# Row sums by ScalarE, a bias added by DMA, a diagonal that turns and scales, and eight dot products in a later stage

## The chip, the cores and the metric

The kernel runs on one core of a Trainium2 chip. The metric is the time of one execution on the device in microseconds, lower is better. The core has five engines that run side by side and meet through semaphores: TensorE (matrix products into PSUM), VectorE, ScalarE (activations, copies with a scale), GpSimd, and SyncE, whose queue (SP) issues most loads. DMAs are issued from the queues of SP, ScalarE and GpSimd.

## The reference

One decoder block over 512 positions with 1024 channels. Two token mixers run on one normed input; the parts that matter here, shortened:

```python
z = h @ w_in                      # a_u, a_v, q, k, v, index parts, gates A and B
mod = silu(c) @ w_ada + b_ada     # six vectors of 1024: shift, scale, gate, twice

# mixer A: gated spatial mixing in chunks of 128 positions, 8 groups
v = layer_norm(gelu(a_v), ln_g, ln_b).reshape(bsz, n, 128, 8, 128)
mixed = einsum('gts,bnsgc->bntgc', w_s * tril, v) + b_s
y_a = gelu(a_u) * mixed

# mixer B: attention over the top 128 keys of an indexer, 8 heads of 128
p = softmax(q @ k_selected);  o = p @ v_selected
merged = sigmoid(g_a) * (y_a @ w_proj_a) + sigmoid(g_b) * (y_b @ w_proj_b)
x = x + gate1 * (merged @ w_out)  # then a SwiGLU block and a norm
```

With the layer norm's offset `ln_b` taken through the mixing, its share is `ln_b` times the row sum of the masked weights; the kernel adds it to the bias.

## The kernel before, in words

The program is one straight list of instructions per engine; their order is that of the calls in the code, without loops on the chip and without a scheduler. The stages follow each other: a first projection (0 to 60 us of the span), q, k, v and the indexer (to 104), a_v (to 156), a_u (to 206), gate A and projection A (to 291), attention together with gate B (to 373), projection B, output projection and the feed-forward block.

Most products run in a split form: an fp32 operand is cut into a high part (ScalarE copies with rounding) and a low part (VectorE or GpSimd subtracts), and `mm3` makes three matmuls of them, high by high, high by low, low by high. Weights come as a list `stream` of 512 KB entries, in the order in which they are made ready. `issue` starts an entry's load into one of three `raw` buffers (`RAWB = 3`), and `room` lets it do so when fewer than three are pending; `prep` makes the high and low part. `get(i, ahead)` makes everything ready up to `ahead` weight chunks further on. A chunk of a_u or gate B has 4 x 128 rows by 256 columns, 24 matmuls of 512 columns.

Between the weight entries stand 24 dot-product entries (kind "m") that make three of the six modulation vectors: rows of `w_ada` are loaded and VectorE forms, in one instruction per 128 outputs (line 209), their product with silu(c) and its sum. `group(..., mods=mm_, nm=...)` puts `nm` of them behind each chunk. With a tile name in `mraw` such an entry has a buffer of its own; with `mraw=False` it shares the three `raw` buffers.

In a_u (`au_tasks` ahead of each chunk's get, `au_post` after its matmuls) VectorE ends the statistics of a_v, ScalarE normalises a_v (`ln_v2`), TensorE makes the mixing products (`mix_mm`, plain fp32), and VectorE combines them with the bias tile `bsb` and with gelu(a_u) (`mix_ev`). The bias tile is loaded by GpSimd as a broadcast to all partitions; the row sums come from a product with a tile of ones (`rs_mm`), and eight VectorE instructions (`bias_mix`) add them, times `ln_b`, to the bias. GpSimd's queue also issues the moves and adding moves of `x_move`, which form sums of weight blocks in DRAM.

In attention there are 16 units of two heads by one block of 128 queries, with four, three, two and one block of keys in turn. In step s unit s has its qk products, mask, maxima (line 1183) and exponentials, unit s-1 its normalisation, unit s-2 is turned (`at_T`) and unit s-3 has its products with v. Between them `gb_part` puts one or two of gate B's 32 steps.

## Time and profile before

| | |
|---|---|
| runs shown | 791.23, 791.38 and 862.42 us, median 791.38 |
| the profiled execution | 791.98 us, its span 790.0 us |
| busy share of the span | TensorE 99%, VectorE 84%, ScalarE 56%, GpSimd 23% |
| DMA | 155.05 MB, mean 196 GB/s |
| granted TensorE clock | 1.00 in each stretch looked at |

The span runs from the first to the last instruction of the program; the execution's own time is 2.0 us longer. A busy share is the time in which an engine has at least one instruction running, over the span. Matmuls overlap each other in the record, so for TensorE the distance between the starts of two neighbours says more than the length of one.

### The profile page before, as it was taken

How to read it: one execution, taken by the hardware profiler on the slowest of the kernel's cores; microseconds unless marked ns; L12 is line 12 of the kernel's file. 1: busy time of each engine (PE TensorE's matmuls, PEld its weight loads, DVE VectorE, ACT ScalarE, POOL GpSimd, SP SyncE). 2: the span in 40 equal slices, each digit the busy share in tenths (PEclk: the TensorE clock that was granted, in tenths of full speed). 3: DMA queues.
4: the chain of work that ended last, by engine and by line, in shares of the span. 5: the costliest groups of instructions: out<-in, count | busy, mean ns of one | idle time of the engine just before them, and what ended most of it. 6: DMA issues, size and time to landing. Idle time of an engine off the chain costs nothing.

```text
span 790.0 us, 12600 instructions
## 1 busy us (share of the span) xinstructions
PE 778.3 (99%) x4747; PEld 694.5 (88%) x4747; DVE 663.7 (84%) x1114; ACT 443.2 (56%) x777; POOL 181.4 (23%) x220
## 2 busy tenths in 40 slices
PE   8999999999999999999999999999999999999996
PEld 6779988878988988988888899999999999878885
DVE  5988887688897799886787879889999888898777
ACT  6556455443362636666536577555665566576654
POOL 2064234574353501000010000313121322100001
PEclk9999999999999999999999999999999999999999
DMA  9959454789763733148692503989998968666664
GB/s 361 416 156 242 119 146 122 217 231 243 212 215 107 235 112 107 54 135 278 232 234 56 187 1 107 255 251 268 258 259 222 260 201 212 177 200 209 209 192 147
DMA packets 89887, 155.05 MB, mean 196 GB/s; under 512 B 7010, under 2 KB 54770, under 8 KB 89635
## 3 DMA queue, kind: packets, MB, share of 16 engines
q1 hardware_dynamic: 72976, 116.05, 44.6%
q0 software_dynamic: 15952, 37.17, 20.9%
q10 hardware_dynamic: 898, 1.04, 0.4%
q8 instruction: 37, 0.61, 0.3%
q14 instruction: 24, 0.19, 0.1%
HBM read 150.16 MB, written 33.56 MB: 233 GB/s over the span
## 4 chain that ended last, share of the span: by engine, by line
PE 64%; DVE 17%; DMA 9%; ACT 5%; issue 4%; POOL 0%; SPq 0%; POOLq 0%; ACTq 0%; DVEq 0%
PE R L66 5%; PE R L68 5%; PE R L67 5%; PE pb L66 5%; PE pb L67 5%; PE pb L68 5%; DMA mraw<-in_w_ada_t_dram 3%; DMA raw<-in_w_ffn_in_dram 3%; DMA raw<-in_w_ffn_out_dram 3%; PE pfo L67 2%; PE pfo L68 2%; PE pfo L66 2%; PE pav L66 2%; PE pav L67 2%; PE pav L68 2%
## 5 line engine op out<-in xcount | busy, mean ns | idle before, releaser
L134 ACT ACTIVATE hi<-raw 128x1024 fp32r<-128x1024 f32 (+1 forms) x111 | 114.5, 1032 | 81.6 <-PE pb L67 32.4
L138 DVE TENSOR_TENSOR lo<-raw,hi 128x1024 fp32r<-128x1024 f32 (+2 forms) x77 | 90.3, 1174 | 26.9 <-ACT hi L134 26.0
L138 POOL TENSOR_TENSOR lo<-raw,hi 128x1024 fp32r<-128x1024 f32 x27 | 69.5, 2577 | 100.2 <-ACT hi L134 69.6
L67 PE MATMUL pfo<-lo,za 128*128 128x512 f32 (+1 forms) x144 | 55.5, 386 | 0.2 <-DVE lo L138 0.2
L66 PE MATMUL pfo<-hi,za 128*128 128x512 f32 (+1 forms) x144 | 55.5, 385 | 0.0
L68 PE MATMUL pfo<-hi,za 128*128 128x512 f32 (+1 forms) x144 | 55.3, 384 | 0.0
L209 DVE CUSTOM_DVE_ANT_0 mraw<-mraw,scb,cols 128x1024 f32<-128x1024 f32 x24 | 37.6, 1568 | 11.7 <-DMA mraw<-in_w_ada_t_dram 11.7
L66 PE MATMUL R<-tb,sx 128*128 128x256 f32 x160 | 45.0, 281 | 0.3 <-ACT gr L462 0.3
L67 PE MATMUL R<-tb,sx 128*128 128x256 f32 x160 | 44.3, 277 | 0.0
L68 PE MATMUL R<-tb,sx 128*128 128x256 f32 x160 | 44.3, 277 | 0.0
L68 PE MATMUL R<-tb,lo 128*128 128x256 f32 x160 | 44.2, 277 | 0.0
L67 PE MATMUL R<-tb,hi 128*128 128x256 f32 x160 | 44.2, 276 | 0.0
L66 PE MATMUL R<-tb,hi 128*128 128x256 f32 x160 | 44.2, 276 | 0.0
L66 PE MATMUL pb<-h,hi 128*128 128x512 f32 (+1 forms) x112 | 42.7, 382 | 0.0
L68 PE MATMUL pb<-h,lo 128*128 128x512 f32 (+1 forms) x112 | 41.9, 374 | 0.0
L67 PE MATMUL pb<-h,hi 128*128 128x512 f32 (+1 forms) x112 | 41.9, 374 | 0.0
L351 POOL COPY sm<-sm 128x1 f32<-128x1 f32 x36 | 23.2, 644 | 78.7 <-ACT sm L350 78.7
L331 POOL DMA_DIRECT2D wsum<-in_w_ffn_out_dram x24 | 21.2, 885 | 78.0 <-DMA wsum<-wsum 46.1
L66 PEld LDWEIGHTS pfo<-hi,za 128*128 128x128 f32 x144 | 27.1, 188 | 6.1 <-ACT ps L1925 0.6
L67 PEld LDWEIGHTS pfo<-lo,za 128*128 128x128 f32 x144 | 27.1, 188 | 6.1 <-DVE lo L138 0.9
L68 PEld LDWEIGHTS pfo<-hi,za 128*128 128x128 f32 x144 | 27.1, 188 | 5.2
L66 PEld LDWEIGHTS R<-tb,sx 128*128 128x128 f32 x160 | 30.1, 188 | 0.9 <-ACT gr L462 0.5
(398 smaller groups left out, 2697.0 us busy)
## 6 DMA issues: line engine op xcount, KB each, us to landing
raw<-in_w_ffn_in_dram SPq DMA_DIRECT2D x44, 512.0 KB, 5.7
raw<-in_w_in_dram SPq DMA_DIRECT2D x30, 512.0 KB, 3.8
wsum<-in_w_ffn_out_dram POOLq DMA_DIRECT2D x30, 512.0 KB, 8.3
mraw<-in_w_ada_t_dram SPq DMA_DIRECT2D x24, 512.0 KB, 6.3
raw<-wsum SPq DMA_DIRECT2D x20, 512.0 KB, 3.8
s<-in_w_ada_t_dram SPq DMA_DIRECT2D x16, 512.0 KB, 8.8
raw<-in_w_ffn_out_dram SPq DMA_DIRECT2D x16, 512.0 KB, 4.6
xsum<-in_w_blocks_dram POOLq DMA_DIRECT2D x12, 512.0 KB, 6.3
```

What stands on the lines that cost most here:

```text
L66: T.matmul(o, wh, rh, start=start, stop=False, **kw)
L67: T.matmul(o, wh, rlo, start=False, stop=False, **kw)
L68: T.matmul(o, wlo, rh, start=False, stop=stop, **kw)
L134: A.activation(hi[:, :m], e["raw"][:, :m], AF.Copy)
L138: e["lo"].tensor_sub(lo[:, :m], e["raw"][:, :m], f(hi[:, :m]))
L209: V.tensor_tensor_reduce(out=raw[:, o], in0=raw[:, o], in1=c, scale=1.0, scalar=col if o.start else bias, op0=OP.mult, op1=OP.add, accum_o ...
L331: P.dma_start(wsum[n][o], src, accum_op=OP.add)
L351: P.tensor_copy(t, t)
```

## The change

Three things are changed.

1. The row sums of the masked spatial weights are made by ScalarE from a second copy of the weights (`gmlp_w_n`, positions in rows; loaded and masked by GpSimd), as the accumulated sum of eight copies. TensorE turns the eight columns, ScalarE copies them out and writes them to DRAM, GpSimd loads them back as a broadcast, ScalarE scales them by `ln_b`, and a DMA of GpSimd adds the bias on top. `rs_mm`, the tile of ones and `bias_mix` are gone.
2. In attention the weights after the exponential are no longer scaled by VectorE. ScalarE makes a diagonal matrix of the inverse sums (`at_diag`, two 128x128 instructions per unit), and the turn is a product with that diagonal in place of a transpose with the identity.
3. The eight dot products that stood between a_u's chunks are gone from there; gate B has two behind each chunk in place of one. All 24 keep their order, so those behind the chunks of projection A are now of the first modulation vector and those of gate B follow on.

```diff
--- before.py
+++ after.py
@@ -27,7 +27,7 @@
 
 @with_exitstack
 def block_kernel(ctx: ExitStack, tc: tile.TileContext, x, x_t, c_row, positions, w_ada_t, w_first, w_in, w_blocks,
-                 gmlp_w_s, gmlp_b_s, w_proj_a, w_proj_b,
+                 gmlp_w_s, gmlp_w_n, gmlp_b_s, w_proj_a, w_proj_b,
                  w_out, w_ffn_in, w_ffn_out, final_norm_g, small, consts, out):
     nc = tc.nc
     T, V, A, P, SY = nc.tensor, nc.vector, nc.scalar, nc.gpsimd, nc.sync
@@ -256,7 +256,7 @@
     mm_ = mods_mid()
     dram = ctx.enter_context(tc.tile_pool(name="dram", bufs=1, space=bass.MemoryType.DRAM))
     W_AV = [[add_w(w_in, [k0, k0 + 1], 1024 + 512 * h, 512, V if k0 % 4 else P) for k0 in range(0, 8, 2)] for h in range(2)]
-    W_AU = [group(w_in, 256 * g, pool=2, mods=mm_, mraw="acc") for g in range(4)]
+    W_AU = [group(w_in, 256 * g, pool=2) for g in range(4)]
     xsum = {(r, n): dram.tile([128, 1024], F32, name=f"xsum{r}{n}") for r in range(2) for n in (1, 2, 3, 4)}
 
     def blk(r, k):
@@ -281,7 +281,7 @@
             W_X[r].append(add_w(b, [0, 1, 2, 3], 0, 256, V if p in (2, 5) else P, 48 if p in (1, 4) else 16))
         for g in (2 * r, 2 * r + 1):
             W_PA.append(group(w_pa, 256 * g, mods=mm_, pool=True, nm=(1 - g % 2,) * 2, mraw=("A2", "A3") if g % 2 == 0 else "A2"))
-    W_GB = [group(w_in, 5192 + 256 * g, pool=2 * (g == 1), mods=mm_, nm=1, mraw=False)
+    W_GB = [group(w_in, 5192 + 256 * g, pool=2 * (g == 1), mods=mm_, nm=2, mraw=False)
             for g in range(4)]
     stream[W_GB[1][0]]["lo"] = V
     W_PB = [group(w_pb, 256 * g, mods=mm_, nm=((0, 1), (1, 1), (1, 0), (0, 0))[g], mraw="k_hi") for g in range(4)]
@@ -296,6 +296,7 @@
     KZ = ([0, 1, 2, 3, 4, 5, 6, 7, 12, 13, 20], [8, 9, 10, 11, 16, 17, 18, 19, 14, 15, 21])
     NZ = 6
 
+    rsd = dram.tile([8, 128], F32, name="rsd")
     wsum = {n: dram.tile([11 * 128, 512], F32, name=f"wsum{n}") for n in (1, 2, 3, 4)}
     gdr = {n: dram.tile([8, 128], F32, name=f"gdr{n}") for n in (2, 5)}
     W_Z = {}
@@ -887,10 +888,37 @@
     vg = []
     late = {}
 
-    def load_bs():
+    def load_wn():
+        late["wn"] = mid.tile([128, 8, 128], F32, name="wn", tag="A1", bufs=1)
+        P.dma_start(late["wn"], gmlp_w_n)
+
+    def mask_wn():
+        P.affine_select(late["wn"], late["wn"], pattern=[[0, 8], [-1, 128]], compare_op=OP.is_ge, fill=0.0, base=0,
+                        channel_multiplier=1)
+
+    def row_sums():
+        for g in range(8):
+            w = late["wn"][:, g]
+            A.activation(w, w, AF.Copy, accum_out=sm[:, g:g + 1])
+
+    def rs_out():
+        p = bank(4, "rsT")
+        T.transpose(p[:8, :128], sm[:, 0:8], ident)
+        gr = tiny.tile([128, 128], F32, name="gr", tag="gr", bufs=1)
+        A.activation(gr[:8], p[:8, :128], AF.Copy)
+        A.dma_start(rsd, gr[:8])
+
+    def rs_in():
         late["bsb"] = mid.tile([128, 8, 128], F32, name="bsb", tag="A3", bufs=1)
-        P.dma_start(late["bsb"], bass.AP(tensor=gmlp_b_s.tensor, offset=gmlp_b_s.offset,
-                                         ap=[[0, 128], [128, 8], [1, 128]]))
+        P.dma_start(late["bsb"].rearrange("p a n -> p (a n)"), rows_bcast(rsd, D))
+
+    def rs_scale():
+        for m in range(8):
+            b = late["bsb"][:, m]
+            A.activation(b, b, AF.Copy, scale=lnbc[:, m:m + 1])
+
+    def add_bs():
+        P.dma_start(late["bsb"].rearrange("p a n -> p (a n)"), rows_bcast(gmlp_b_s, D), accum_op=OP.add)
 
     def load_ws():
         late["wmT"] = mid.tile([128, 8, 128], F32, name="wmT", tag="A2", bufs=1)
@@ -899,15 +927,13 @@
     def mask_ws():
         P.affine_select(late["wmT"], late["wmT"], pattern=[[0, 8], [1, 128]], compare_op=OP.is_ge, fill=0.0, base=0,
                         channel_multiplier=-1)
-        late["ones"] = mid.tile([128, 2, 128], F32, name="ones2", tag="ql", bufs=2)[:, 0]
-        P.memset(late["ones"], 1.0)
 
     VT = {0: [load_ws, lambda: rows_a(1), lambda: rows_b(1)],
-          1: [lambda: h_hi("S1"), lambda: h_hi("S4"), lambda: h_lo("S1"), lambda: h_lo("S4")],
+          1: [load_wn, lambda: h_hi("S1"), lambda: h_hi("S4"), lambda: h_lo("S1"), lambda: h_lo("S4")],
           2: [lambda: rows_a(2), lambda: rows_b(2), lambda: h_hi("S3")],
-          3: [lambda: h_lo("S3")],
-          5: [mask_ws],
-          7: [load_bs]}
+          3: [lambda: h_lo("S3"), mask_wn],
+          4: [row_sums],
+          5: [mask_ws]}
     for _ in range(16):
         bg.append((1.4, topk_max))
         bg.append((1.4, topk_replace))
@@ -940,6 +966,8 @@
             for tk in range(4):
                 opt_a_mm(pb[tk], tk, hi, lo, stream[i]["kts"], hT, 8)
             idx_mms(4 if vs > 2 else 3)
+            if vs == 7:
+                rs_out()
         if not vg:
             vg.extend(mid.tile([128, 2, D], F32, name=f"vg{i}", tag=f"P{i}", bufs=1) for i in range(2))
         for tk in range(4):
@@ -980,17 +1008,6 @@
             ylow.append(lambda: V.tensor_sub(yT[m][1], y, f(yT[m][0])))
         ylate.append((austep[0] - 1, hi))
 
-    def rs_mm():
-        late["rs"] = [bank(5 + k, "rs") for k in range(2)]
-        for k, p in enumerate(late["rs"]):
-            T.matmul(p, late["ones"], late["wmT"][:, 4 * k:4 * k + 4].rearrange("p a n -> p (a n)"), start=True, stop=True)
-
-    def bias_mix():
-        for m in range(8):
-            b = late["bsb"][:, m]
-            V.scalar_tensor_tensor(b, late["rs"][m // 4][:, 128 * (m % 4):128 * (m % 4) + 128], lnbc[:, m:m + 1], b,
-                                   op0=OP.mult, op1=OP.add)
-
     ub = {}
     austep = [0, 0]
     AT = {3: [0], 4: [1, 2], 5: [3], 6: [4], 7: [5], 8: [6], 9: [7]}
@@ -998,8 +1015,6 @@
     def au_post():
         s = austep[1]
         austep[1] += 1
-        if s == 2:
-            rs_mm()
         for m in AT.get(s, []):
             mix_mm(m)
         while ylate and ylate[0][0] < s:
@@ -1014,11 +1029,14 @@
                 ln_v(tk, 1)
             rstd(rva, mva[:, :, 1], 4, 1.0)
             V.scalar_tensor_tensor(nmr, mva[:, :, 0], -1.0, rva, op0=OP.mult, op1=OP.mult)
+            rs_in()
         elif s < 3:
+            if s == 1:
+                rs_scale()
+            else:
+                add_bs()
             ln_v2(2 * s - 2)
             ln_v2(2 * s - 1)
-        elif s == 3:
-            bias_mix()
         while ylow:
             ylow.pop(0)()
         for m in AT.get(s - 1, []):
@@ -1198,8 +1216,16 @@
         n = (i + 1) * 128
         pt, mx = AS["p", u]
         V.reciprocal(mx[:, 6:8], mx[:, 4:6])
+
+    dgs = []
+
+    def at_diag(u):
+        if not dgs:
+            dgs.append(base.tile([128, 4, 2, 128], F32, name="dg", tag="hs4", bufs=1))
+        mx = AS["p", u][1]
+        AS["d", u] = dgs[0][:, u % 4]
         for e in range(2):
-            V.tensor_scalar(pt[e][:, :n], pt[e][:, :n], mx[:, 6 + e:7 + e], None, op0=OP.mult)
+            A.activation(AS["d", u][:, e], ident, AF.Copy, scale=mx[:, 6 + e:7 + e])
 
     def at_T(u):
         i, hp = aun[u]
@@ -1213,8 +1239,8 @@
             p = bank(4 + s0 // 2, "pT")
             for s in range(ns):
                 for e in range(2):
-                    T.transpose(p[:, (s * 2 + e) * 128:(s * 2 + e + 1) * 128],
-                                pt[e][:, (s0 + s) * 128:(s0 + s + 1) * 128], ident)
+                    T.matmul(p[:, (s * 2 + e) * 128:(s * 2 + e + 1) * 128],
+                             pt[e][:, (s0 + s) * 128:(s0 + s + 1) * 128], AS["d", u][:, e], start=True, stop=True)
             o = th[:, s0:s0 + ns].rearrange("p s e n -> p (s e n)")
             ol = tl[:, s0:s0 + ns].rearrange("p s e n -> p (s e n)")
             ev.append((o, ol, p[:, :ns * 256]))
@@ -1277,6 +1303,8 @@
         low = at_split(s + 2, True) if 0 < s < NU - 2 else lambda: None
         if s < NU:
             at_exp(s)
+        if 1 <= s <= NU:
+            at_diag(s - 1)
         low()
         gb_part(GBN[s], 2 if s else 1)
     mbank[0] = 6
...
     given["gmlp_w_s"] = _np.asarray(inputs["gmlp_w_s"])[0].transpose(2, 0, 1)
+    given["gmlp_w_n"] = _np.asarray(inputs["gmlp_w_s"])[0].transpose(1, 0, 2)
     for name in _INS:
         a = _np.ascontiguousarray(given[name])
         arrays[f"in_{name}_dram"] = a
```

On ScalarE, at the start of a_u: the rows from the high part of a_u's second chunk (the first row) to the high part of its fourth (the last). `vg` is a_v, `pav` its PSUM banks, `bsb` the bias tile.

```order
L134 ACTIVATE hi<-raw 128x1024 [waits DMAHW2_49,Pool_49]
L946 ACTIVATE vg_1305<-pav 128x512 [waits PE_49] x2
L946 ACTIVATE vg_1306<-pav 128x512 [waits PE_49] x2
L134 ACTIVATE hi<-raw 128x1024 [waits DMAHW4_49]
L952 ACTIVATE vg_1305<-vg_1305,sm 128x1024 [waits DVE_49,Activation_49]
L952 ACTIVATE vg_1305<-vg_1305,sm 128x1024 [waits Activation_49]
L134 ACTIVATE hi<-raw 128x1024 [waits DMAHW5_49,PE_49]
```

And in the changed kernel:

```order
L134 ACTIVATE hi<-raw 128x1024 [waits DMAHW2_49,Pool_49]
L974 ACTIVATE vg_1309<-pav 128x512 [waits PE_49] x2
L974 ACTIVATE vg_1310<-pav 128x512 [waits PE_49] x2
L134 ACTIVATE hi<-raw 128x1024 [waits DMAHW3_49]
L918 ACTIVATE bsb<-bsb,cols 128x128 [waits DMASW0_49]
L918 ACTIVATE bsb<-bsb,cols 128x128 x7
L980 ACTIVATE vg_1309<-vg_1309,sm 128x1024 [waits DVE_49,Activation_49]
L980 ACTIVATE vg_1309<-vg_1309,sm 128x1024 [waits Activation_49]
L134 ACTIVATE hi<-raw 128x1024 [waits DMAHW4_49,PE_49]
```

The eight scalings, which wait for the broadcast's DMA, stand ahead of two normalisations and of the fourth chunk's high part.

On SP's queue, from the last load of projection A to the fifth load of gate B's stage; `raw<-in_w_in` is a weight chunk of gate B, `raw<-in_w_ada` a dot-product entry.

```order
L115 DMA raw<-in_w_proj_a_dram 128x4x256 [waits DMAHW6_49,Pool_49]
L205 DMA mraw<-in_w_ada_t_dram 128x1024
L115 DMA raw<-in_w_in_dram 128x4x256 [waits DMAHW7_49,DVE_49]
L205 DMA raw<-in_w_ada_t_dram 128x1024 [waits DMAHW1_49,Pool_49]
L115 DMA raw<-in_w_in_dram 128x4x256 [waits DMAHW2_49,DVE_49]
L205 DMA raw<-in_w_ada_t_dram 128x1024 [waits DMAHW4_49,DVE_49]
L115 DMA raw<-in_w_in_dram 128x4x256 [waits DMAHW0_49,DVE_49]
```

And in the changed kernel:

```order
L115 DMA raw<-in_w_proj_a_dram 128x4x256 [waits DMAHW6_49,Pool_49]
L205 DMA mraw<-in_w_ada_t_dram 128x1024
L115 DMA raw<-in_w_in_dram 128x4x256 [waits DMAHW7_49,DVE_49]
L205 DMA raw<-in_w_ada_t_dram 128x1024 [waits DMAHW1_49,Pool_49]
L205 DMA raw<-in_w_ada_t_dram 128x1024 [waits DMAHW2_49,DVE_49]
L115 DMA raw<-in_w_in_dram 128x4x256 [waits DMAHW4_49,DVE_49]
L205 DMA raw<-in_w_ada_t_dram 128x1024 [waits DMAHW0_49,DVE_49]
```

The second weight chunk of gate B is the fourth load into the three buffers, where it was the third; its wait on VectorE is that for the low part of the first chunk.

On VectorE, from the low part of gate B's first chunk (the first row) to the first unit's maxima (the last rows, `pt,mx<-qk`):

```order
L138 TENSOR_TENSOR lo<-raw,hi 128x1024
L773 TENSOR_SCALAR sco_639<-sco_639 128x384
L773 TENSOR_SCALAR sco_638<-sco_638 128x256
L1070 TENSOR_TENSOR ql<-qf_615,qh 128x256
L209 ISA raw,Gc<-raw,scb,cols 128x1024
L209 ISA Gc 128x1
L138 TENSOR_TENSOR lo<-raw,hi 128x1024
L1183 ISA pt,mx<-qk,sco_640 128x512
```

And in the changed kernel:

```order
L138 TENSOR_TENSOR lo<-raw,hi 128x1024
L774 TENSOR_SCALAR sco_640<-sco_640 128x384
L774 TENSOR_SCALAR sco_639<-sco_639 128x256
L1088 TENSOR_TENSOR ql<-qf_616,qh 128x256
L209 ISA raw,GG_88<-raw,scb,cols 128x1024
L209 ISA GG_88 128x1
L209 ISA raw,GG_88<-raw,scb,cols 128x1024
L209 ISA GG_88 128x1
L138 TENSOR_TENSOR lo<-raw,hi 128x1024
L1201 ISA pt,mx<-qk,sco_641 128x512
```

A second dot product stands ahead of the second chunk's low part, and the first unit's maxima stand behind that low part in both.

## Rows read from the trace of the kernel before

**Rows 1.** The page, busy times of the engines (us, share of the span, instructions):

```profile
PE 778.3 (99%) x4747; PEld 694.5 (88%) x4747; DVE 663.7 (84%) x1114; ACT 443.2 (56%) x777; POOL 181.4 (23%) x220
```

**Rows 2.** Stages: length, PE, PEld, DVE, ACT, POOL busy, clock, DMA share, GB/s:

```profile
110.00:155.00 45.00, 44.98 (x209) 37.74 (x208) 33.77 (x47) 22.55 (x40) 22.71 (x23) 1.00 0.60 156
155.00:222.00 67.00, 67.00 (x383) 58.29 (x383) 55.69 (x98) 30.06 (x40) 34.39 (x22) 1.00 0.80 221
...
290.00:372.00 82.00, 81.89 (x482) 72.39 (x481) 69.53 (x203) 51.31 (x128) 5.59 (x5) 1.00 0.45 146
```

**Rows 3.** Waits of TensorE's matmuls, longest first (us in total, times, longest):

```profile
PE warm L492 <- POOL ones L382: 2.4, 1, 2.4
...
PE zx L1116 <- DVE zx L1126: 0.4, 1, 0.4
```

**Rows 4.** Timeline of TensorE around the ones-product (start, us, engine, line, names):

```profile
172.04 0.39 PE L68 MATMUL pb<-h,lo 128*128 128x512 f32 x1
172.27 1.88 PE L986 MATMUL rs<-wmT,ones 128*128 128x512 f32 x4
...
174.22 0.40 PE L67 MATMUL pb<-h,hi 128*128 128x512 f32 x1
```

**Rows 5.** The same around the first mixing product:

```profile
179.48 1.05 PE L965 MATMUL mix<-wmT,vg 128*128 128x128 f32 x8
...
180.60 0.40 PE L67 MATMUL pb<-h,hi 128*128 128x512 f32 x1
```

**Rows 6.** The same around one unit's transposes:

```profile
311.00 1.04 PE L1216 MATMUL pT<-ident,pt 128*128 128x128 f32 x8
...
312.10 0.39 PE L67 MATMUL pgb<-h,hi 128*128 128x512 f32 x1
```

**Rows 7.** Groups of VectorE, 290 to 372 us (count, busy us, mean ns, idle before):

```profile
L1202 DVE TENSOR_SCALAR pt<-pt,mx 128x512 f32<-128x512 f32 (+3 forms) x32 | 10.9, 384 | 0.6
L209 DVE CUSTOM_DVE_ANT_0 raw<-raw,scb,cols 128x1024 f32<-128x1024 f32 x8 | 10.2, 1280 | 0.0
```

**Rows 8.** Timeline of ScalarE, exponentials of a unit with one key block:

```profile
351.71 0.40 ACT L1193 ACTIVATE pt<-pt,mx 128x128 f32<-128x128 f32 x1
352.02 0.19 ACT L1193 ACTIVATION_READ_ACCUMULATOR pt<-pt,mx 128x1 f32 x1
352.11 0.39 ACT L1193 ACTIVATE pt<-pt,mx 128x128 f32<-128x128 f32 x1
```

**Rows 9.** Timeline of ScalarE and GpSimd at the start of a_u:

```profile
159.10 1.13 POOL L268 DMA_DIRECT2D xsum<-in_w_blocks_dram  x1
...
159.42 2.38 ACT L952 ACTIVATE vg<-vg,sm 128x1024 f32<-128x1024 f32 x2 [1.73 <-DVE sm L1016]
...
170.91 2.40 POOL L138 TENSOR_TENSOR lo<-raw,hi 128x1024 fp32r<-128x1024 f32 x1 [4.30 <-ACT hi L134]
```

**Rows 10.** DMA issues (queue, count, KB each, median us from issue to landing):

```profile
xsum<-in_w_blocks_dram POOLq DMA_DIRECT2D x12, 512.0 KB, 6.3
...
raw<-in_w_ada_t_dram SPq DMA_DIRECT2D x8, 512.0 KB, 4.4
...
bsb<-in_gmlp_b_s_dram POOLq DMA_DIRECT2D x1, 512.0 KB, 5.1
```

**Rows 11.** Timeline of SP's queue, ScalarE, VectorE and TensorE at gate B's start:

```profile
283.82 0.37 SPq L115 DMA_DIRECT2D raw<-in_w_in_dram  x1
...
287.60 1.06 ACT L134 ACTIVATE hi<-raw 128x1024 fp32r<-128x1024 f32 x1 [5.81 <-DMA raw<-in_w_in_dram]
...
288.40 0.34 SPq L205 DMA_DIRECT2D raw<-in_w_ada_t_dram  x1
...
290.30 1.23 DVE L138 TENSOR_TENSOR lo<-raw,hi 128x1024 fp32r<-128x1024 f32 x1
...
292.20 0.69 DVE L1183 CUSTOM_DVE_ANT_0 pt<-qk,sco 128x512 f32<-128x512 f32 x1 [0.68 <-PE qk L68]
...
294.04 0.39 PE L66 MATMUL qk<-k_hi,qh 128*128 128x512 f32 x1
```

More of the change, by code (lines that the diff above doesn't have):

```diff
@@ L2026, in block_kernel @@
                 finish(tk)
-_INS = ["x", "x_t", "c_row", "positions", "w_ada_t", "w_first", "w_in", "w_blocks", "gmlp_w_s", "gmlp_b_s",
+_INS = ["x", "x_t", "c_row", "positions", "w_ada_t", "w_first", "w_in", "w_blocks", "gmlp_w_s", "gmlp_w_n", "gmlp_b_s",
         "w_proj_a", "w_proj_b", "w_out", "w_ffn_in", "w_ffn_out", "final_norm_g", "small", "consts"]
```

## The prediction

> **What bounds the kernel now.** I read the busy times first, then the stages, then what TensorE waited for, then single rows at the places the diff touches. TensorE is busy for 778.3 us, 99% of the span [rows 1], in the two stages concerned for 67.00 of 67.00 and 81.89 of 82.00 us, at a granted clock of 1.00, while VectorE has 55.69 and 69.53 [rows 2]. Busy time alone could hide stretched matmuls, so the second look is at waits: once the first projection runs, no wait of a matmul is longer than 0.4 us, and that one is on the sum of a Strassen block [rows 3]. The third look is at starts: 512-column matmuls start 0.23 us apart, right up to the next kind of work [rows 4]. So TensorE's issue is the limit, stage by stage. Work taken off VectorE or ScalarE is worth nothing where no matmul waits for it; work put on TensorE costs its full length; a new wait costs what exceeds its slack. I therefore price TensorE rows in full and everything else by slack.
>
> **Turning with the diagonal.** The two scalings per unit leave VectorE: 32 rows, 10.9 us of its time [rows 7]. ScalarE makes 32 diagonals, 128x128, instead; the nearest row is the exponential of that shape, 0.31 us up to its accumulator read [rows 8], so 9.9 us on an engine with 51.31 of 82 us busy. The transposes become real matmuls of fp32 data. A transpose is one row of the trace: 80 rows for 80 blocks, 8 of them from 311.00 until the next 512-column matmul but one, 312.10, less its 0.23, so 311.87: 0.109 us each [rows 6]. The spatial mixing has the same shape, fp32 by fp32; the code makes four calls per group and the trace has eight rows, from 179.48 to 180.60 - 0.23 = 180.37, 0.111 us each [rows 5]: a true fp32 product is two rows. TensorE therefore gets 160 x 0.111 - 80 x 0.109 = 17.8 - 8.7 = **+9.1 us**, all on the path that sets the end, with no cover. This is the largest term and the best founded one.
>
> **Row sums.** The ones-product goes: four rows from 172.27 to 174.22 - 0.23 = 173.99, **-1.7 us** on TensorE [rows 4]. One 8-column transpose comes, at most one row of the turning kind, +0.1. The eight combinations that leave VectorE are no gain by themselves. On ScalarE the eight row sums are 8 x 0.40 = 3.2 us [rows 8] at step 4 of a_v; it is busy for 22.55 of 45 us in that stretch, so the relu rows behind them move into pauses: 0 to 0.5 us, I take 0. The masking of the second copy is one more pass on GpSimd, which has 22.71 us to do there [rows 2]. The sums' way through DRAM ends before GpSimd reaches the broadcast.
>
> The new wait is in a_u. GpSimd issues the broadcast where it now issues a weight-sum move, 159.10 [rows 9]; the bias load of the same size took 5.1 us [rows 10], so it lands near 164.2. ScalarE stands waiting in front of it, and behind it in its queue are two normalisations and the high part of a_u's fourth chunk. 8 x 0.31 = 2.5 us of scaling end at 166.7, the two normalisations take 2.4, to 169.1, the high part 1.06 [rows 11], to 170.1, GpSimd's low part 2.40, to 172.5. TensorE comes to that chunk at 172.27 (where the ones-product stood) and to its low part two matmuls later, at 172.7. So the slack of some 8 us that these steps had is just used up: nothing with these values, 1.0 us with the broadcast at the 6.3 us of GpSimd's other moves [rows 10]. I take **+0.2**. The adding DMA stands behind that low part on GpSimd, with a weight-sum move and the next low part behind it; at 6.3 us it lands near 179, when its reader's other input, the first mixing product at 179.48 [rows 5], is only being made: 0.
>
> **The dot products.** VectorE loses 8 x 1.28 us in a_u and the waits for their loads, and gets as many back in gate B [rows 7], where 10.9 us have left. The 0.4 us wait at the end of a_u, behind late VectorE work [rows 3], should go: **-0.4**, between 0 and twice that.
>
> What is dear is the order of the loads. The three raw buffers take gate B's first chunk, then two dot-product rows, and the second weight chunk must wait until the first chunk's low part has freed a buffer. Its load was issued at 283.82 and used at 287.60; now it takes the place of the load at 288.40 [rows 11]. With the same 3.8 us it lands at 292.2, its high part ends at 293.3, its low part (1.23) at 294.5. VectorE stands in front of that low part, and behind it is the first unit's softmax, which started at 292.20. Its first half (0.69) reads the bank that the second unit's qk wants: that started at 294.04 and can now start at 294.5 + 0.7 = 295.2, **+1.2 us**. The first turn also comes later, since its diagonal stands on ScalarE behind the second unit's exponentials: of the 2.3 us by which the softmax is late TensorE has then lost 1.2, so up to 1.1 us more, **+0.4** if a good half of that was slack. Together 1.6; with a load of 3.0 us 0.8, with one of 6.3 us 4.1. From then on a unit has more TensorE work and no more VectorE work, so the pipeline catches up and I expect nothing further. Later loads have a whole chunk's time.
>
> **Sum.** 9.1 - 1.7 + 0.1 + 0.2 - 0.4 + 1.6 = +8.9 us. The profiled execution took 791.98 us (790.0 of span and 2.0 around it), so 800.9; the runs shown at 791.23 and 791.38 are some 0.6 lower: **800.3 us**, 1.1% above the median.
>
> **A rule weighed.** The rows say that TensorE has no room in the attention stage: 81.89 of 82.00 us busy and no wait over 0.4 us [rows 2, 3]. The Trainium skill, Perfetto Trace Analysis, section Identifying the Most-Contended Engine, says that matmul busy time measures the nearness to the limit badly, and that the busy share of the weight loads does it well. By that rule 72.39 of 82.00 us leave 9.6 us of room in the stage, and the sum would be 800.3 - 9.1 = 791.2. I trust the starts of the matmuls: 481 weight loads in 72.39 us are 0.15 us each, under the 0.23 us of a 512-column stream, so full issue already shows as less than full load time.
>
> **Rivals.** *The extra TensorE rows fit into pauses* (chance 0.07). For it: VectorE had 85% of the stage, and with 10.9 us off it the units could close up. Against: rows 2, 3 and 4. The 9.1 us fall away, 791.2, and if the late start is absorbed too, 789.6. This is where the rule above would lead.
>
> *The diagonal product is one row per block, as the transpose was* (0.04), so that the change costs less than the code seems to say. For it: same shape, same stationary operand. Against: two rows per call in the mixing. Price: again without the 9.1, 791.2.
>
> *Loads in gate B bind chunk after chunk* (0.07), the case that ends slower by over 2%. Place: the raw buffers, where a chunk's load starts only after the last chunk's low part. Cycle: landing + 1.06 + 1.23. Per chunk TensorE has 24 x 0.23 = 5.5 us of gate and two units; counted in rows of 0.11 us, a unit with one key block has 11 of them and a chunk there 7.9 us, one with two blocks 20 and 9.9 us, and the mean over the stage is (82.0 + 9.1) / 8 = 11.4. At 3.8 us of landing the cycle is 6.1 and hides; it decides from 5.6 us on in the shortest units. At 10 us it is 12.3 and costs 2 x 4.4 + 2 x 2.4 = 13.6 us more, 813.9. For it: 24 loads instead of 16 in this stage, and moves of 6.3 us elsewhere. Against: a DMA share of 0.45 in the stage [rows 2], and dot-product loads that land in 4.4 us there [rows 10].
>
> **How the numbers follow.** The forecast has 0.82, the rivals 0.07, 0.04 and 0.07. The low end takes 0.8 off for the wait at the end of a_u, 0.8 for the start and 0 in a_u: 9.1 - 1.7 - 0.8 + 0.1 + 0.8 = 7.5, 798.8; I set it at 797, for small stretches of matmuls in the attention stage that VectorE's relief may shorten and that no row sums up. The high end takes 0.5 in a_v, 1.0 in a_u, 4.1 at the start and no gain on the wait: 9.1 - 1.7 + 0.1 + 0.5 + 1.0 + 4.1 = 13.1, 804.4, with the same margin up 806. Range **797 to 806**. Two per cent, about what a measurement of this kernel tells from no change, is 15.8 us, 807.2: slower by over that 0.07, faster by over that 0.01, within 0.92.
>
> **What would show it.** Right: 160 rows of the turning product, about 0.111 us apart; no rows of the ones-product; a VectorE with more idle time in a_u and as much work as before in gate B; one wait of about 1 us at the second unit's qk, with load, high part, low part and softmax before it; the fourth chunk of a_u with no wait above 1 us. Wrong: 80 turning rows, or an attention stage lengthened by much less than 9 us; waits of TensorE spread over all chunks of gate B; a span that shrinks though TensorE's rows grew.

## The result, and the profile after

The changed kernel took 801.4 us in the median of four runs (801.31 to 802.36), the kernel before 791.6 on the same chip: a ratio of 1.0128, 95% interval 1.0108 to 1.0148, so 9.8 us more. One of the four runs of the kernel before took 862.42 us; it counts in that median and not in the ratio. 800.3 was predicted. The profiled execution has a span of 800.4 us, 10.4 more than before.

The page's busy times:

```profile
PE 786.6 (98%) x4824; PEld 703.7 (88%) x4824; DVE 653.4 (82%) x1074; ACT 456.8 (57%) x834; POOL 182.8 (23%) x222
```

The stages of [rows 2], with the same columns:

```profile
110.00:156.00 46.00, 44.54 (x208) 37.30 (x207) 34.62 (x43) 25.02 (x56) 23.36 (x23) 1.00 0.54 136
156.00:223.00 67.00, 67.00 (x392) 59.15 (x391) 46.42 (x82) 33.57 (x49) 36.57 (x25) 1.00 0.76 197
290.00:383.00 93.00, 91.28 (x558) 80.81 (x557) 66.85 (x185) 61.58 (x162) 4.63 (x5) 1.00 0.51 165
```

TensorE has 77 rows more than in [rows 1]: 80 for the turn, one transpose of the sums, less the four of the ones-product. The attention stretch is 93 us long here and was 82 in [rows 2]; both begin and end at chosen whole microseconds, and the starts of the matmuls, below, give 12.1 us of growth. In a_u VectorE lost 9 us of work and TensorE stayed full. TensorE now has pauses in a_v and in attention, which the waits name (us in total, times, longest):

```profile
PE pav L66 <- ACT vg L974: 1.5, 1, 1.5
PE pv L67 <- DVE tl L1300: 1.1, 2, 0.6
...
PE pT L1242 <- ACT dg L1228: 0.4, 1, 0.4
```

The `zx` wait of [rows 3] is gone. The turn of one unit, in the timeline of TensorE (start, us, engine, line, names):

```profile
313.01 1.95 PE L1242 MATMUL pT<-dg,pt 128*128 128x128 f32 x16
314.80 0.27 PE L461 MATMUL mod<-ident,GG 128*8 128x128 f32 x1
```

Where [rows 6] had eight rows there are sixteen, and the next start is 1.79 us later: 0.112 us a row, close to the 0.111 that the prediction took from the mixing.

**The a_v pause.** Rows of GpSimd, VectorE, ScalarE and TensorE (a bracket holds the idle time before and what ended it):

```profile
113.79 0.57 POOL L893 DMA_DIRECT2D wn<-in_gmlp_w_n_dram  x1
...
115.03 1.00 POOL L753 MEMSET sco<- 128x512 f32 x1
...
126.96 2.08 POOL L896 TENSOR_SCALAR_AFFINE_SELECT wn<-wn 128x1024 f32<-128x1024 f32 x1
...
128.00 2.44 DVE L754 SCALAR_TENSOR_TENSOR sco<-rl,wi,sco 128x512 f32<-128x512 f32 x2
...
132.43 2.07 ACT L974 ACTIVATE vg<-pav 128x512 f32<-128x512 f32 x4
133.08 0.50 PE L66 MATMUL pav<-hi,h 128*128 128x512 f32 x1 [1.46 <-ACT vg L974]
```

The two VectorE rows in the kernel before:

```profile
127.15 1.60 DVE L753 SCALAR_TENSOR_TENSOR sco<-rl,wi,sco 128x512 f32<-128x512 f32 x2
```

The issue of the second copy's load takes GpSimd 0.57 us, and behind it stands a fill for which VectorE's index sums wait: 1.91 us, where it was 1.34. Then the mask runs beside two rows of those sums, which take 2.44 us in place of 1.60. 0.57 and 0.84 make 1.41; ScalarE's gelu is late by about that, and TensorE waits 1.46 us for PSUM banks. The 0.84 is taken up by an experiment below; the 0.57 is read from this trace alone, since no kernel here has the load's issue elsewhere.

**a_u.** ScalarE at the fourth chunk, GpSimd behind it:

```profile
165.32 2.45 ACT L918 ACTIVATE bsb<-bsb,cols 128x128 f32<-128x128 f32 x8 [5.82 <-DMA bsb<-rsd]
167.68 2.37 ACT L980 ACTIVATE vg<-vg,sm 128x1024 f32<-128x1024 f32 x2
169.95 1.04 ACT L134 ACTIVATE hi<-raw 128x1024 fp32r<-128x1024 f32 x1
...
171.07 2.41 POOL L138 TENSOR_TENSOR lo<-raw,hi 128x1024 fp32r<-128x1024 f32 x1 [5.38 <-ACT hi L134]
173.42 0.92 POOL L921 DMA_DIRECT2D bsb<-in_gmlp_b_s_dram  x1
```

The prediction had these steps at 164.2, 166.7, 169.1 and 170.1; they came up to 1.1 us late, but so did TensorE after a_v, and no matmul waits.

**Attention's ends.** SP's queue, ScalarE, VectorE and TensorE, first at the start and then at the end of the stage:

```profile
286.94 0.38 SPq L115 DMA_DIRECT2D raw<-in_w_in_dram  x1
...
290.49 1.06 ACT L134 ACTIVATE hi<-raw 128x1024 fp32r<-128x1024 f32 x1 [9.46 <-DMA raw<-in_w_in_dram]
...
292.72 0.68 DVE L1201 CUSTOM_DVE_ANT_0 pt<-qk,sco 128x512 f32<-128x512 f32 x1
...
293.56 0.47 PE L66 MATMUL qk<-k_hi,qh 128*128 128x512 f32 x1
...
361.85 1.53 SPq L205 DMA_DIRECT2D raw<-in_w_ada_t_dram  x2
364.19 7.93 SPq L115 DMA_DIRECT2D raw<-in_w_proj_b_dram  x3
...
372.47 1.06 ACT L134 ACTIVATE hi<-raw 128x1024 fp32r<-128x1024 f32 x1 [2.03 <-DMA raw<-in_w_proj_b_dram]
373.56 1.23 DVE L138 TENSOR_TENSOR lo<-raw,hi 128x1024 fp32r<-128x1024 f32 x1 [1.84 <-ACT hi L134]
...
374.70 0.42 DVE L1290 TENSOR_TENSOR yb<-pv,yb 128x256 fp32r<-128x256 f32 x1
...
375.65 0.42 DVE L1300 TENSOR_TENSOR tl<-pT,th 128x256 fp32r<-128x256 f32 x1
...
376.12 0.39 PE L67 MATMUL pv<-tl,v_hi 128*128 128x256 f32 x1 [0.50 <-DVE tl L1300]
```

At the start the load that [rows 11] had at 283.82 comes at 286.94, the first maxima 0.52 us later than there, the second unit's qk 0.48 earlier. At the end the first chunk of projection B is issued behind two dot-product loads and lands 8.3 us after its issue. ScalarE waits 2.03 us in front of its high part, VectorE 1.84 us in front of its low part. Behind that low part VectorE has, without a gap, `yb` of a finished unit, the maxima of another and then `tl`, for which TensorE waits. ScalarE's copies behind the high part end at 374.1, before `tl` starts, so here the lateness passes through VectorE's queue.

The starts of the same matmuls in both traces, after minus before, show where the time goes: +0.26 us since the start-up, +1.80 at the end of a_v, +0.04 past the place of the ones-product, -0.75 in gate A, +11.37 at the end of attention, +10.44 near the end of the program. So attention alone has 12.1 of it.

### The profile page after: what moved, and what is told of

Same layout as the page of the kernel before. It is cut to its first block, busy times and chain, and to the rows that moved or that the text cites. A ratio compares the mean times of both kernels' runs of the same rounds, so it can differ in the third digit from the quotient of the medians.

```text
span 800.4 us, 12771 instructions
## 1 busy us (share of the span) xinstructions
PE 786.6 (98%) x4824; PEld 703.7 (88%) x4824; DVE 653.4 (82%) x1074; ACT 456.8 (57%) x834; POOL 182.8 (23%) x222
## 4 chain that ended last, share of the span: by engine, by line
PE 77%; DVE 11%; ACT 5%; DMA 4%; issue 2%; POOL 0%; POOLq 0%; ACTq 0%; DVEq 0%; SPq 0%
PE R L66 7%; PE R L68 7%; PE R L67 7%; PE pb L67 6%; PE pb L66 6%; PE pb L68 6%; PE pfo L66 4%; PE pfo L67 4%; PE pfo L68 4%; PE zx L1135 2%; PE zx L1137 2%; PE pT L1242 2%; PE zx L1134 2%; PE o L551 1%; PE o L553 1%
## 5 line engine op out<-in xcount | busy, mean ns | idle before, releaser
L138 POOL TENSOR_TENSOR lo<-raw,hi 128x1024 fp32r<-128x1024 f32 x27 | 67.4, 2497 | 94.0 <-ACT hi L134 85.6
L66 PEld LDWEIGHTS R<-tb,sx 128*128 128x128 f32 x160 | 30.1, 188 | 1.3 <-ACT R L1848 0.7
L67 PEld LDWEIGHTS R<-tb,sx 128*128 128x128 f32 x160 | 30.1, 188 | 0.0
```

The lines of the kernel that those rows point to most:

```text
L66: T.matmul(o, wh, rh, start=start, stop=False, **kw)
L67: T.matmul(o, wh, rlo, start=False, stop=False, **kw)
L138: e["lo"].tensor_sub(lo[:, :m], e["raw"][:, :m], f(hi[:, :m]))
```

## The experiments

The experiments ran in three groups of four kernels, each beside the kernel before, which took 791.69, 793.02 and 792.24 us there; so ratios are compared.

**Each part alone.** `e1_diag`, `e2_rows` and `e3_dots` are the kernel before with the hunks of part 2 (diagonal), part 1 (row sums) and part 3 (dot products) of the diff above. `e4_ident` keeps VectorE's scaling and has only

```diff
-                    T.transpose(p[:, ...], pt[e][:, ...], ident)
+                    T.matmul(p[:, ...], pt[e][:, ...], ident, start=True, stop=True)
```

Expected of `e1_diag`: 

> The kernel before with the turning part of the change alone. Theory A (the trace of after read as: 9.1 us of new TensorE rows, and separate stalls that belong to the row sums and to the loads of the dot products): 791.6 + 9.1 = 800.7 us, 800.2 to 801.4, with no wait of TensorE over 0.5 us in attention. Rival B (the stalls at both ends of the attention stage come from the diagonal, which ScalarE makes late): 9.1 + 1.4 + 2.0, 804 us, with waits on the diagonal or on the low part of the turned weights. Rival C (a good part of the new rows fits into pauses, and after is slow for other reasons): below 798 us.

Expected of `e4_ident`: 

> The kernel before, VectorE's scaling kept, and the 80 transposes made true products with the identity: the same result, TensorE's rows of the change and nothing else of it. Theory A: 160 rows of 0.111 us in place of 80 of 0.109, +9.1, 800.7 us, the same as with the diagonal to within 0.5 us. Rival B: the same 800.7, but the kernel with the diagonal 2 us or more behind it. Rival C: below 798 us.

Expected of `e2_rows`: 

> The kernel before with the row sums part alone. Theory A (the second mask on GpSimd delays the index sums, through them ScalarE's gelu of a_v, and so TensorE's second half of a_v by 1.5 us, which eats the gain of the ones-product): -1.7 + 0.1 + 1.5, so 791.5 us, 791.2 to 792.0, with one wait of TensorE of 1.3 to 1.7 us on the gelu of a_v. Rival: the stall in a_v belongs to another part or to chance, 790.0 us and no such wait.

Expected of `e3_dots`: 

> The kernel before with the eight dot products moved, alone. Theory A (two dot products ahead of a weight chunk in three load buffers make the chunk late at the start of attention, 1.4 us, and at its end, 2.0 us, and the wait at the end of a_u goes, -0.8): 791.6 + 2.6 = 794.2 us, 793 to 796, with waits at the first turn and at the last units. Rival B (those two stalls come from the diagonal): 790.8 us, no wait over 0.5 us in attention. Rival D (with the shorter units of before the loads bind chunk after chunk): over 797 us.

Measured: diagonal 801.41 us, 1.0116 (1.0099 to 1.0133); identity 801.78, 1.0120 (1.0102 to 1.0138). They agree, and neither has a wait of TensorE in attention. By the starts of the matmuls the stage grew by 8.77 us with the diagonal (from +0.29 to +9.06 against before) and by 8.78 with the identity (+0.64 to +9.42). The same window of both, diagonal first:

```profile
290.00:382.00 92.00, 92.00 (x569) 82.68 (x568) 59.66 (x171) 61.37 (x162) 4.60 (x5) 1.00 0.42 130
```

```profile
290.00:382.00 92.00, 92.00 (x568) 82.63 (x567) 70.70 (x203) 51.77 (x129) 5.28 (x5) 1.00 0.43 135
```

VectorE has 11 us less to do in the first, and TensorE is full in both: the cost is TensorE's rows, and B and C fall.

The other two went far past what was expected. Row sums alone: 797.65 us, 1.0067 (1.0050 to 1.0085), where 791.5 was expected. Dot products alone: 799.84, 1.0101 (1.0078 to 1.0124), above D's 797, where A had 794.2. The longest waits of the row sums alone, after that of the start-up:

```profile
PE zx L1134 <- ACT zx L1121: 2.0, 1, 2.0
PE pav L66 <- ACT vg L974: 1.4, 1, 1.4
...
PE zx L1134 <- ACT u L1065: 0.7, 1, 0.7
PE mix L993 <- DVE y L1001: 0.6, 1, 0.6
```

Two stretches of it (columns as in [rows 2]), and its median landing of the dot-product loads between 155 and 200 us (the last number), with that of the kernel before under it:

```profile
222.00:224.50 2.50, 1.24 (x9) 1.24 (x10) 2.36 (x3) 2.50 (x4) 1.70 (x1) 0.95 0.07 28
224.50:227.80 3.30, 3.30 (x17) 3.19 (x15) 3.30 (x4) 3.27 (x5) 0.71 (x1) 0.52 0.36 124
```

```profile
mraw<-in_w_ada_t_dram SPq DMA_DIRECT2D x6, 512.0 KB, 6.3
mraw<-in_w_ada_t_dram SPq DMA_DIRECT2D x6, 512.0 KB, 5.4
```

The a_v pause is there as expected. The rest arises at the start of gate A. In a_u the eight dot products share one buffer of their own, so load, dot product and the next load form a chain. A landing takes 6.3 us here where the kernel before has 5.4. The first dot product is 2.5 us late (TensorE itself 1.6), the last one starts at 211.44 in place of 205.30. VectorE's mixing stands behind them; TensorE waits 3.3 us in three places, and after the longest pause its granted clock is 0.52 for 3.3 us, some 1.7 us more. On the way to that pause stands one more delay, a row of the mixing beside GpSimd's low part:

```profile
217.03 2.39 POOL L138 TENSOR_TENSOR lo<-raw,hi 128x1024 fp32r<-128x1024 f32 x1 [6.84 <-ACT hi L134]
217.76 2.20 DVE L1004 TENSOR_TENSOR y<-y,u 128x512 f32<-128x512 f32 x1
```

That row takes 0.69 us where no such low part runs beside it. Three of the eight rows of this kind are stretched so here, one in the kernel before. How much of the 6 us belongs to this and how much to the loads was not separated.

With the dot products alone the waits stand in attention, most of them in its first quarter and two smaller ones (0.3 and 0.5 us) at its end:

```profile
PE pv L67 <- DVE tl L1274: 3.5, 3, 1.9
...
PE qk L66 <- DVE mx L1183: 0.9, 1, 0.9
```

The longest of them in the timeline of SP's queue, ScalarE and TensorE:

```profile
303.13 0.38 SPq L115 DMA_DIRECT2D raw<-in_w_in_dram  x1
...
308.26 1.06 ACT L134 ACTIVATE hi<-raw 128x1024 fp32r<-128x1024 f32 x1 [2.18 <-DMA raw<-in_w_in_dram]
309.23 0.37 ACT L1263 ACTIVATE yb<-pv 128x256 fp32r<-128x256 f32 x1
309.49 1.08 ACT L1273 ACTIVATE th<-pT 128x512 fp32r<-128x512 f32 x2
...
312.44 0.39 PE L67 MATMUL pv<-tl,v_hi 128*128 128x256 f32 x1 [1.90 <-DVE tl L1274]
```

A chunk's load stands behind two dot products and ScalarE waits at the high part, as at the end of the stage after the change; here the lateness goes on through the copies `yb` and `th` behind it, then VectorE's `tl`, then TensorE. VectorE is a rival: it is busy for 12.7 of the 13 us from 300 to 313 (12.6 in the kernel before, 10.8 in the changed one), ended two dot products of its own at 309.45, only 0.17 us before ScalarE's copy reached it, and the wait at 305 us has VectorE's rows alone in its chain, without a late load. The time is that of Rival D, the picture isn't: between 316 and 363 us TensorE waits for nothing, so the loads don't bind chunk after chunk.

**The parts in pairs.** The three parts alone cost 9.7 + 6.0 + 8.1 = 23.8 us, together 9.8. `p12`, `p13` and `p23` have two parts each, by their numbers.

Expected of `p12`: 

> Row sums and turning product together, the dot products left in a_u. The row sums alone cost 6.0 us and the turning product alone 9.7. Theory A (the row sums' 6 us arise in a_u, where two more 512 KB DMAs for the bias slow the chain of dot-product loads, and have nothing to do with attention): the two add up, 791.6 + 15.7 = 807.3 us, 805.5 to 809. Rival (the 6 us were chance, or come back in attention): 800 to 802.

Expected of `p13`: 

> Row sums and moved dot products together, transposes and VectorE's scaling as before. Theory A (moving the dot products takes away what made the row sums dear in a_u, leaving -1.7 + 0.1 + 1.5 there; in attention nothing covers the dot products): -0.1 + 8.1, 799.6 us, 798 to 801. Rival (each part's cost is its own): 6.0 + 8.1, 805.7.

Expected of `p23`: 

> Turning product and moved dot products together, row sums as before. Theory A (the product takes 10.9 us off VectorE and makes the units longer, so that the dot products cost only the two stalls seen at the ends of the stage): 9.1 + 1.4 + 2.0 - 0.8, 803.3 us, 801.5 to 804.5. Rival (each part's cost is its own): 9.7 + 8.1, 809.4.

Measured: `p12` 807.42 us, 1.0202 (1.0177 to 1.0227), +15.2; `p13` 798.69, 1.0083 (1.0068 to 1.0098), +6.5; `p23` 802.57, 1.0134 (1.0115 to 1.0153), +10.3. All three came as theory A had it, and each rival misses by 5 us or more. So the costs of row sums and diagonal add up; moving the dot products takes away what made the row sums dear (the waits at gate A are gone in `p13`); and the diagonal takes away most of what makes the moved dot products dear in attention. By the starts attention grows by 8.6 us with the moved dot products alone, and with both by 11.3, 2.5 more than with the diagonal alone. The diagonal lengthens the units and also frees VectorE; identity product and moved dot products together, which would tell the two apart, were not run.

**The mask later.** The changed kernel with

```diff
-          3: [lambda: h_lo("S3"), mask_wn],
-          4: [row_sums],
+          3: [lambda: h_lo("S3")],
+          4: [mask_wn, row_sums],
```

Expected: 

> The changed kernel with the mask of the second weight copy one step later in a_v, behind the index part's pass and fill on GpSimd, where GpSimd then waits 8 us for a high part. Theory A (the mask stands ahead of work that ScalarE's gelu waits for): TensorE's 1.5 us wait in a_v goes, 801.4 - 1.5 = 799.9 us. Rival: the gelu is late for another reason (the load of the second copy, ScalarE's own queue), the wait stays and the time is 801.4.

Measured: 802.31 us, 1.0120 (1.0095 to 1.0145), which tells neither theory A (1.0105 or so) from the rival (1.0128): both lie in the interval. The trace shows what moved:

```profile
128.53 1.60 DVE L754 SCALAR_TENSOR_TENSOR sco<-rl,wi,sco 128x512 f32<-128x512 f32 x2
...
130.82 1.09 POOL L896 TENSOR_SCALAR_AFFINE_SELECT wn<-wn 128x1024 f32<-128x1024 f32 x1
...
132.76 0.50 PE L66 MATMUL pav<-hi,h 128*128 128x512 f32 x1 [0.60 <-ACT vg L974]
```

The two index rows are at 1.60 us again, and TensorE's wait has gone from 1.46 to 0.60, about the 0.57 of the load's issue, which stayed; that the rest is this issue fits, but no run moves it. The theory's account was half right: the mask was the cause, but it did not stand in the way in GpSimd's queue, it slowed VectorE's rows beside it.

**ScalarE scales, TensorE transposes.** The changed kernel, in which ScalarE multiplies the weights themselves:

```diff
-            A.activation(AS["d", u][:, e], ident, AF.Copy, scale=mx[:, 6 + e:7 + e])
+            A.activation(pt[e][:, :n], pt[e][:, :n], AF.Copy, scale=mx[:, 6 + e:7 + e])
...
-                    T.matmul(p[:, ...], pt[e][:, ...], AS["d", u][:, e], start=True, stop=True)
+                    T.transpose(p[:, ...], pt[e][:, ...], ident)
```

Expected: 

> The changed kernel with transposes again in place of the products with the diagonal, and ScalarE, not VectorE, scaling the weights. VectorE is relieved as in the change, but TensorE gets no new rows. Theory A (the cost of the diagonal is its 9.1 us of TensorE rows and nothing else): 801.4 - 9.1 = 792.3 us, 791.5 to 793.5. Rival E (the longer units of the diagonal also gave the weight loads and VectorE time, so that without them the two dot products behind each chunk bind): 795 to 798, with waits of TensorE in attention like those of the kernel with the moved dot products alone. Rival F (ScalarE becomes late by the wider scalings): over 798, with waits on the exponentials or the high parts.

Measured: 796.77 us, 1.0060 (1.0037 to 1.0082): 0.67% less than the changed kernel, where theory A wanted 1.1%. The time is that of Rival E. Its longest waits of TensorE in attention are 1.3 us at a qk and 1.6 us at `pv`, both early in the stage, where the changed kernel has 0.6 us at most: without the extra rows the units are shorter, and the loads are late again. A part is Rival F's: TensorE waits 0.7 us in two turns for ScalarE's scalings, and at 300 us such scalings stand ahead of a high part for which VectorE waits 0.96 us. The two parts were not separated.

**Lighter ends.** The changed kernel with

```diff
-W_GB: nm=2
+W_GB: nm=((1, 2), (2, 2), (2, 2), (2, 1))[g]
-W_PB: nm=((0, 1), (1, 1), (1, 0), (0, 0))[g]
+W_PB: nm=((0, 1), (1, 1), (1, 1), (1, 0))[g]
```

Expected: 

> The changed kernel with one dot product instead of two behind the first and the last weight chunk of gate B; the two go to projection B, into its own buffer. Theory A (the stall at the start of attention, 1.4 us, and at its end, 2.0 us, are made by weight loads that stand behind dot products in the three buffers): 801.4 - 3.4 = 798.0 us, 797.5 to 799, and no wait over 0.5 us in attention. Rival (they come from the diagonal, or from DMAs that are slow anyway): the waits stay, 801 us.

Measured: 806.21 us, 1.0177 (1.0147 to 1.0208), slower: both expected times, 798.0 and 801, were missed. The mechanism of theory A was right for attention: no wait is left there, and it grew by 9.1 us against before, 3.0 less than in the changed kernel. But the two dot products cost more where they went. The waits that are new, in projection B and behind it:

```profile
PE pb L68 <- DVE lo L138: 1.2, 1, 1.2
PE po L66 <- ACT po L1553: 0.9, 1, 0.9
```

VectorE waits 4.3 us for such a dot product's load there, with the low part queued behind it; between 400 and 480 us of the span 4.9 us are lost against the changed kernel.

**All three edits,** `e8_all`. Expected: 

> All three edits together: the mask later, ScalarE scaling with transposes, one dot product at the first and last chunk. Theory A: 801.4 - 1.5 - 9.1 - 3.4 = 787.4 us, 787 to 789, under the kernel before by 0.3 to 0.6%. Rival E (dot products bind in the shorter units): 790 to 794.

Measured: 799.27 us, 1.0077 (1.0052 to 1.0101), so both expectations were missed. Attention ends 9.4 us earlier than in the changed kernel; 3.9 of them are given back by 440 us, with a wait of 2.3 us for a low part in projection B, and 2.3 are left near the end of the program. Neither gate B nor projection B took the moved dot products for nothing.

**Row sums early.** The kernel before with part 1, the mask later as above, and

```diff
+          7: [rs_in]}          # a_v, last step; was: a_u, first step
...
+            rs_scale()         # a_u, first step; was: second
...
+            if s == 1:
+                add_bs()       # second; was: third
```

Expected: 

> The kernel before with the row sums part alone, but with the second mask one step later and the whole way of the bias some 6 us earlier: the broadcast is issued in the last step of a_v, ScalarE scales at the first step of a_u, the adding DMA comes at the second. Theory A (with the row sums alone the bias DMAs come between the dot-product loads of a_u; earlier they meet an emptier DMA stretch, and the mask's stall shrinks to 0.6 us): -1.7 + 0.1 + 0.6, 790.6 us, 790 to 792. Rival (any two more 512 KB DMAs in this stretch delay the chain of loads, wherever they stand): 794 to 798 us, with late dot products and waits of TensorE at the start of gate A again.

Measured: 794.26 us, 1.0025 (1.0012 to 1.0038): the low end of the rival's range, with the rival's signs. It is 0.4% better than the row sums alone and still behind the kernel before. Its waits:

```profile
PE zx L1133 <- ACT zx L1120: 2.0, 1, 2.0
PE mix L994 <- DVE y L1002: 1.1, 1, 1.1
PE pav L66 <- ACT vg L975: 0.6, 1, 0.6
```

The last dot product still starts at 210.37. By the starts gate A costs 5.2 us, against 5.8 with the row sums alone, so the place of the bias DMAs is the smaller part of it. Which of the added DMAs makes the chain late is not settled: the second copy's load, the broadcast and the add were not tried one by one. No version here beats the kernel before.

## Why the prediction held, and where it didn't

- **Turning, +9.1.** This term was right and the best founded: there are 160 rows of 0.112 us, and the stage is longer by 8.77 and 8.78 us in the two kernels in which TensorE's work changes in nothing else. The 0.3 us under the estimate lie between 307 and 309 us, where the kernel before lost some time and both gain it back. The price came from the mixing's rows; the code alone shows as many calls as before.
- **Ones-product, -1.7.** This term was right: between the starts on both sides of its place there are 1.76 us less.
- **a_v, 0.** This step failed. It asked whether GpSimd had time for one more pass, and it had. What counted was which rows of VectorE ran beside that pass (0.84 us) and what stood behind the load's issue in GpSimd's queue (0.57 us), a row that the prediction did not price at all. TensorE lost 1.46 us by the two.
- **a_u, +0.2 for the broadcast and 0 for the adding DMA.** The changed kernel has no wait here: the broadcast landed at 165.29 us and the adding DMA at 180.34, for 164.2 and about 179. But TensorE itself came 1.8 us late, which widened the slack, and the 0 held only because part 3 had emptied the stretch of eight loads: with the dot products in place (`e2_rows`, `p12`) the same part costs 6 us. The prediction gave the cover (the mixing product is only being made) and didn't ask what else the DMAs slow.
- **The wait at the end of a_u, -0.4.** It measured -0.79, inside its bounds, and its account is borne out with one exception: the gain stands in all eight kernels here that move the dot products out of a_u, and `e2_rows`, `e4_ident`, `p12` and `e9_early`, which leave them there, still have the wait. The exception is `e1_diag`, which leaves them there too and gained 0.63 us; its last dot product started 1.5 us earlier than in the kernel before, and why stays open.
- **Gate B's start, +1.6.** This term was too large. Against `e7_ends`, which has one dot product at the start, the changed kernel is 0.5 us later by 300 us. The wait of about 1 us at the second unit's qk, which was to show it, came as 0.4 us between starts. The chain was right, its first time wasn't: the load was issued at 286.94, not where [rows 11] had 288.40, since the low part that frees its buffer ended 1.5 us earlier.
- **"The pipeline catches up, expect nothing further."** This step failed. Against `e7_ends` the changed kernel loses 0.6 us more by 312 us and 1.9 in the stage's last units. The forecast held that later loads have a whole chunk's time; at the end the load of projection B's first chunk landed 8.3 us after its issue, past the 5.6 us from which the rival of loads that bind lets them decide in the shortest units. The cycle is that rival's, landing, high part, low part; what it left out is the work queued behind the low part on VectorE (`yb`, maxima, `tl`). In the middle of the stage the lateness goes another way: at 310 us a load that landed in 4.85 us made ScalarE wait 1.31 us at the high part, with a copy behind it, and VectorE's `yb`, maxima and `tl` behind that. The loads did not bind chunk after chunk in the changed kernel. Its units are longer by the diagonal's rows and its VectorE is freer; in `e3_dots`, with neither, and in `e6_act`, with a freer VectorE alone, TensorE waits early in the stage.
- **The other rivals.** The extra rows did not fit into pauses: with them alone TensorE is busy for 92.00 of 92.00 us. The product is not one row per block: the trace has 160 rows for 80 blocks.
- **The rule on weight loads.** The Trainium skill (Perfetto Trace Analysis, section Identifying the Most-Contended Engine) calls the busy time of the matmuls a poor measure of how near TensorE is to its limit and takes the busy share of the weight loads instead. The trace does not bear it out here. [Rows 2] left 9.6 us of the stage without a weight load, and `e1_diag` still leaves 9.3 of 92.00, so the added rows found no room in that share. By the rule the diagonal alone would have cost about nothing, an estimate from those 9.6 us; `e1_diag` took 801.4 us, 9.7 more than the kernel before, and decides against it.

So the total was near for a good reason in its largest term and by offset in the small ones. From the predicted +8.9 to the span's +10.4 the steps are +1.5 for a_v, -1.1 at gate B's start, +2.5 later in attention (drift of some tenths included), -0.4 at the end of a_u, -0.2 in a_u, and -0.7 in the start-up and behind attention, where the change touches nothing.

## What to carry to other kernels

A part that is priced at nothing because something hides it has a price that belongs to the whole change: three parts here cost 23.8 us one by one and 9.8 together, since one empties the stretch that another fills, and one lengthens the units that cover another's loads and frees the engine that works on them. When a tuned kernel's first engine never waits, rows added to it can be priced to a few tenths of a microsecond (9.1 forecast, 8.8 measured), while work moved between the other engines is decided by what stands behind it in each queue and runs beside it. Before moving loads to a stretch with room, look for the engine that will wait in front of them, and list what stands behind that wait in its queue.

## What the runs showed of the hardware

- **GpSimd and VectorE slow each other.** The mask of 128x1024 took 2.08 us in the changed kernel, and the two index rows beside it 2.44, where they take 1.60 alone. One step later (`e5_mask`) the mask took 1.09 us, and VectorE's two rows beside it 2.15 in place of 1.34, but TensorE did not wait for those. In `e2_rows` a 128x512 product of two tiles on VectorE took 2.20 us beside GpSimd's low part of 128x1024, and takes 0.69 alone.
- **After some pauses of TensorE the granted clock falls.** Past the start-up it fell to its lower level, 1.2 GHz, for 3.4 us after pauses of 1.99 (`e2_rows`), 1.90 (`e3_dots`), 1.99 (`p12`) and 1.99 us (`e9_early`), and 256-column matmuls then started 0.21 us apart in place of 0.115. It did not fall after 1.89 (`p13`), 1.87 (`p12`) and 2.32 us (`e8_all`), nor after the 1.46 us of the changed kernel. So in these traces a pause of about 2 us sometimes cost some 1.7 us more, and what decides stays open.
